# Gate and up projections by seven products of quarters instead of eight, in a two-layer decoder trunk

## The chip, the core and the metric

The kernel runs on one core of a Trainium2 chip. The metric is the device time of one execution in microseconds; lower is better. The core has five engines that run their own queues of instructions in order and wait for one another through semaphores: TensorE (PE in the profile; its weight loads are PEld), VectorE (DVE), ScalarE (ACT), GpSimd (POOL) and SyncE (SP), which here only issues DMA transfers. Matmul results land in PSUM, in 8 banks of 128 x 512 fp32; everything else lives in SBUF, in tiles of 128 partitions.

## The reference

One sequence of 512 tokens of width 1024 goes through two layers. Layer 0 mixes tokens with a short gated convolution and sliding-window attention, layer 1 with gated linear attention and latent attention. Each mixer is followed by a layer norm of `ALPHA * x + y`, by a SwiGLU feed-forward part of width 2816, and by another layer norm. The change concerns the feed-forward part:

```python
def swiglu(x, w_gate, w_up, w_down):
    return (jax.nn.silu(x @ w_gate) * (x @ w_up)) @ w_down
```

with x of 512 x 1024, `w_gate` and `w_up` of 1024 x 2816 and `w_down` of 2816 x 1024, all fp32.

## The kernel before

**Products in three passes.** TensorE multiplies in the type float32r, which holds fewer bits than fp32. So each fp32 operand is split in a high and a low part: `split` rounds it on ScalarE (`hi`), and takes `src - hi` on VectorE (`lo`), or on GpSimd for the first three weights after a `down`. A product is then hi·hi + hi·lo + lo·hi, three matmuls.

**Weights** lie in one DRAM tensor as pieces of 128 x 1024 fp32 (512 KB) in the order of their use. `weight()` loads the next piece into a `raw` tile (pool of 5; issued on SP) and splits it into a `w` tile (pool of 5, each with both parts). A load waits for its `raw` tile to be free, that is for the split of an earlier weight.

**Input of the feed-forward part.** `layer_norm` makes one block of 128 tokens at a time, and its `flip` transposes the block on TensorE (8 transposes into two PSUM tiles). ScalarE casts them to `xh` and VectorE makes `xl`: both hold x transposed, 128 x 8 x 512 (features k of the input in eights, tokens along the row). The norm's reciprocal root, `rs`, is a pow on GpSimd.

**Gate and up** (`ffn`). 22 feature tiles of 128 features; each needs a gate and an up product, and each of these 8 (k) x 3 matmuls of 512 columns (`gemm_a`), whose lhsT is 128 x 128 of the weight and whose rhs is `xh` or `xl`. Tiles 0 and 1 run in two halves of 256 tokens, so that the first halves can start while the last two blocks of the norm are still being made: with the first halves are woven the flips of the third and fourth block. `finish` makes the hidden tile `h` = silu(gate) · up with a tanh on ScalarE and two operations on VectorE.

**Down.** For each of the 22 hidden tiles, split on the way into two `hx` tiles, 4 x 2 x 3 matmuls of 512 columns; then the norm.

**Order.** Only TensorE's queue follows the order of the program's text. For the other engines a scheduler decides, by the dependencies and its own costs, before the program is built.

**Names.** `wk` are 14 slots, which hold hidden tiles; `m8` is one tile of 8 x 512 that holds the mixer's output and then eight hidden tiles; `tmp` and `p` are temporaries of four buffers each; `ps` are PSUM banks. Lines that matter below: L176 matmuls of `gemm_a`; L281 matmuls of `down`; L94 and L100 the two parts of `split`, L98 its GpSimd form; L231 to L255 the norm, with L249 the pow and L255 its last step; L263 to L268 the flip.

Of the kernel before, what the change touches and what calls it, by code (L numbers as in the profile page):

```python
# [10 lines left out]
F32 = mybir.dt.float32  # L11
F32R = mybir.dt.float32r
# [20 lines left out]
WARM = 8  # L33
RAW, WP, WK, HX = 5, 5, 14, 11
LEVELS = (64, 32, 16, 8, 4, 2, 1)
# [8 lines left out]
def trunk(ctx, tc, a, out):  # L44
# [31 lines left out]

    def small(shape, tag):
        return sm.tile(shape, F32, tag=tag, name=nm(tag))

# [44 lines left out]
    def begin(banks):  # L124
# [98 lines left out]

    def layer_norm(b, acc, gb, last):

# [33 lines left out]
        def flip():  # L259
            for h in range(2):  # L260
                tp = ps()
                for k in range(4):
                    nc.tensor.transpose(tp[:, k * P:(k + 1) * P],  # L263
                                        xn[:, b, h * 512 + k * P:h * 512 + (k + 1) * P], ident)
                tv = tp.rearrange("p (k t) -> p k t", k=4)
                dst = (slice(None), slice(4 * h, 4 * h + 4), slice(b * P, (b + 1) * P))
                nc.scalar.copy(out=xh[dst], in_=tv)
                tt(out=xl[dst], in0=tv, in1=xh[dst].bitcast(F32), op=ALU.subtract)  # L268
        return flip

    def down(hs, groups, gb, last=False, after=None):

# [18 lines left out]
        for gi, size in enumerate(groups):  # L291
            parts = [prep(k) for k in range(k0, k0 + size)]
            k0 += size
            for b in range(NB):
                if gi == 0:
                    acc[b] = [ps(), ps()]
                todo = [(part, h) for part in parts for h in range(2)]
                if k0 == nk:
                    todo.sort(key=lambda x: x[1])
                for n, ((k, hh, hl, w), h) in enumerate(todo):  # L300
                    if n == 6 * len(todo) // 10 and k0 == nk and b >= 2 and not last:
                        flips.pop(0)()
                    one(k, b, h, hh, hl, w)
                if gi == 0 and after:
                    after.pop(0)()
                if k0 == nk:
                    flips.append(layer_norm(b, acc[b], gb, last))
        state["pool"] = POOL
        return flips

    def ffn(layer, last, flips):
        gb = load_ln("ffn", layer)
        m8 = big.tile([P, 8, S], F32, tag="m8", name=nm("m8"))
        hs = []

        def finish(f, pg, pu):
            h = m8[:, f, :] if f < 8 else slot()
            t = temp()
# [7 lines left out]
        for f in range(2):  # L326
            for part in range(2):
# [4 lines left out]
                gemm_a(bank, w, cols=slice(0, 256), ks=range(4, KD))  # L332
                first.append((w, bank))
        for f in range(2):
            for w, bank in first[2 * f:2 * f + 2]:
                gemm_a(bank, w, cols=slice(256, 512))
            finish(f, first[2 * f][1], first[2 * f + 1][1])
        with tc.issue_after(norm.ins):
            w = weight()
        for f in range(2, KF):  # L340
            pg, pu = ps(), ps()
            gemm_a(pg, w or weight())
            w = None
            gemm_a(pu, weight())
            finish(f, pg, pu)
        return down(hs, [1] * (KF - 5) + [5], gb, last)


    def mixer0():
# [120 lines left out]
        weave(att[1:], fill[4:])  # L470
        return down([mix[:, i, :] for i in (4, 5, 6, 7, 0, 1, 2, 3)], [4, 4], gb)

# [8 lines left out]
    def mixer1(flips):  # L481
# [7 lines left out]
        def latent(b, bank):  # L489
# [352 lines left out]
        for c in range(3):  # L842
# [11 lines left out]
        return down([mix[:, i, :] for i in (4, 5, 6, 7, 0, 1, 2, 3)], [4, 4], gb,  # L854
                    after=[lambda: output_flip(2), lambda: output_flip(3)])

# [26 lines left out]
def _chunks(w_in0, w_out0, w_in1, w_out1, wg, wu, wd, uq, ukv):  # L883
# [120 lines left out]
```

## Time and profile before

| | |
|---|---|
| median of 3 runs | 1114.32 us (1113.13 to 1114.58) |
| profiled execution | 1115.11 us, its span 1113.3 us |
| TensorE | busy 1098.2 us (99%), 5488 matmuls |
| VectorE | 549.7 us (49%) |
| ScalarE | 374.3 us (34%) |
| GpSimd | 79.3 us (7%) |
| DMA | 109.18 MB, mean 98 GB/s |

"Busy" counts the time in which an engine has an instruction running. Matmuls overlap in the array, so that the mean length of one is longer than the pitch at which they follow one another; how fast they run is read from their starts. A chain of work, followed back from the last instruction, tells which engine's time made the end.

### The profile page before, as it was taken

To read this page: it belongs to the slowest core of one execution; us is meant where nothing else is said; L and a number is where in the kernel's file an instruction comes from. 1 tells how busy PE (TensorE), PEld (TensorE's weight loads), DVE (VectorE), ACT (ScalarE), POOL (GpSimd) and SP (SyncE) were. 2 spreads that over 40 slices of the span, in tenths; PEclk is the share of its full clock that TensorE was granted. 3 is DMA by queue.
4 is the path that set the end of the run, shared out by engine and by line. 5 is a ranking of instruction groups with operands and counts; after the bars stand their busy time and mean duration, and the time that the engine had idled before them with its cause. 6 is when DMAs were issued, how large, how long until landed. Compare 5 with 4: busy or idle time off the path is not lost.

```text
span 1113.3 us, 13695 instructions
## 1 busy us (share of the span) xinstructions
PE 1098.2 (99%) x5488; PEld 918.8 (83%) x5488; DVE 549.7 (49%) x910; ACT 374.3 (34%) x656; POOL 79.3 (7%) x108
## 2 busy tenths in 40 slices
PE   9999999999999999999999999999999999999997
PEld 7888889888888888888987788889888888888885
DVE  5666458433333333334857885485433333333337
ACT  4543343322222222323466444343322222223321
POOL 0000013000000000000513411130000000000001
PEclk9999999999999999999999999999999999999999
DMA  9512223422222322221341030314222223232202
GB/s 353 180 64 77 76 76 114 133 95 94 95 98 94 108 99 95 95 95 57 95 152 58 1 115 9 122 59 170 96 95 95 95 95 102 95 106 96 95 1 76
DMA packets 31487, 109.18 MB, mean 98 GB/s; under 512 B 3504, under 2 KB 3648, under 8 KB 31424
## 3 DMA queue, kind: packets, MB, share of 16 engines
q1 hardware_dynamic: 31424, 108.31, 28.8%
q8 instruction: 43, 0.70, 0.3%
q14 instruction: 20, 0.16, 0.1%
HBM read 106.20 MB, written 2.10 MB: 97 GB/s over the span
## 4 chain that ended last, share of the span: by engine, by line
PE 91%; DVE 6%; ACT 1%; issue 1%; DMA 0%; POOL 0%; DVEq 0%; SPq 0%; ACTq 0%; POOLq 0%
PE ps L176 52%; PE ps L281 26%; PE ps L210 6%; DVE xn L255 1%; PE ps L733 1%; DVE p L252 1%; DVE p L231 1%; PE ps L657 1%; DVE xl L268 1%; PE ps L431 1%; PE ps L378 1%; PE ps L418 1%; DVE w L100 1%; DVE st L234 1%; PE ps L785 0%
## 5 line engine op out<-in xcount | busy, mean ns | idle before, releaser
L176 PE MATMUL ps<-xh,w 128*128 128x512 f32 (+1 forms) x1888 | 556.9, 377 | 0.8 <-ACT xh L94 0.8
L176 PEld LDWEIGHTS ps<-xh,w 128*128 128x128 f32 x1888 | 347.5, 189 | 66.2 <-ACT xh L94 1.5
L176 PE MATMUL ps<-xl,w 128*128 128x512 f32 (+1 forms) x944 | 354.9, 376 | 0.5 <-DVE xl L268 0.5
L281 PE MATMUL ps<-w,hx 128*128 128x512 f32 x1440 | 329.4, 390 | 0.0
L281 PEld LDWEIGHTS ps<-w,hx 128*128 128x128 f32 x1440 | 269.7, 188 | 55.6
L94 ACT CAST w<-raw 128x1024 fp32r<-128x1024 f32 (+2 forms) x184 | 189.8, 1039 | 343.5 <-PE ps L281 160.4
L100 DVE TENSOR_TENSOR w<-raw,w 128x1024 fp32r<-128x1024 f32 (+1 forms) x175 | 212.6, 1218 | 73.2 <-ACT w L94 68.7
L176 PEld LDWEIGHTS ps<-xl,w 128*128 128x128 f32 x944 | 178.3, 189 | 32.8 <-DVE xl L268 0.9
L320 DVE SCALAR_TENSOR_TENSOR tmp<-tmp,ps 128x512 f32<-128x512 f32 x44 | 30.3, 688 | 152.2 <-ACT tmp L319 152.2
L319 ACT ACTIVATE tmp<-ps 128x512 f32<-128x512 f32 x44 | 26.3, 598 | 180.4 <-PE ps L176 180.4
L249 POOL TENSOR_TENSOR rs<-ve,neghalf 128x1 f32<-128x1 f32 x16 | 11.5, 719 | 741.8 <-DVE ve L247 711.3
L100 DVE TENSOR_TENSOR hx<-wk,hx 128x512 fp32r<-128x512 f32 x28 | 19.4, 692 | 82.8 <-PE ps L281 82.8
L210 PE MATMUL ps<-w,xh 128*128 128x512 f32 (+1 forms) x192 | 58.1, 383 | 0.0
L321 DVE SCALAR_TENSOR_TENSOR wk<-tmp,ps 128x512 f32<-128x512 f32 x28 | 19.3, 688 | 74.1 <-PE ps L176 74.1
L100 DVE TENSOR_TENSOR hx<-m,hx 128x512 fp32r<-128x512 f32 x32 | 21.7, 686 | 45.8 <-PE ps L281 37.5
L210 PEld LDWEIGHTS ps<-w,xh 128*128 128x128 f32 x192 | 35.5, 188 | 5.3
L98 POOL TENSOR_TENSOR w<-raw,w 128x512 fp32r<-128x512 f32 (+1 forms) x18 | 28.1, 1594 | 154.9 <-ACT w L94 153.1
L210 PE MATMUL ps<-w,xl 128*128 128x512 f32 (+1 forms) x96 | 36.3, 378 | 0.0
L231 DVE SCALAR_TENSOR_TENSOR p<-xn,ps 128x512 f32<-128x512 f32 x32 | 21.8, 680 | 15.6 <-PE ps L281 15.6
L252 DVE SCALAR_TENSOR_TENSOR p<-p,neg,lng 128x512 f32<-128x512 f32 x32 | 25.8, 826 | 5.9 <-ACT ps L245 5.9
L255 DVE SCALAR_TENSOR_TENSOR xn<-p,rs,lnb 128x512 f32<-128x512 f32 x32 | 26.7, 876 | 2.0 <-POOL rs L249 1.4
L321 DVE SCALAR_TENSOR_TENSOR m<-tmp,ps 128x512 f32<-128x512 f32 x16 | 11.0, 688 | 32.1 <-PE ps L176 31.8
(178 smaller groups left out, 650.4 us busy)
## 6 DMA issues: line engine op xcount, KB each, us to landing
raw<-in_w_dram SPq DMA_DIRECT2D x182, 512.0 KB, 3.6
hx<-in_xT_dram SPq DMA_DIRECT2D x8, 256.0 KB, 5.5
xn<-in_xn_dram SPq DMA_DIRECT2D x4, 512.0 KB, 8.4
out_dram<-xn SPq DMA_DIRECT2D x8, 256.0 KB, 2.0
raw<-in_w_dram SPq DMA_DIRECT2D x4, 256.0 KB, 5.2
lng<-in_ln_mix_g_dram SPq DMA_DIRECT2D x2, 512.0 KB, 6.8
lnb<-in_ln_mix_b_dram SPq DMA_DIRECT2D x2, 512.0 KB, 6.8
lng<-in_ln_ffn_g_dram SPq DMA_DIRECT2D x2, 512.0 KB, 4.4
```

The lines of the kernel that those rows point to most:

```text
L94: nc.scalar.copy(out=hi, in_=src)
L98: nc.gpsimd.tensor_tensor(out=lo[:, c], in0=src[:, c], in1=hi[:, c].bitcast(F32), op=ALU.subtract)
L100: tt(out=lo, in0=src, in1=hi.bitcast(F32), op=ALU.subtract)
L176: mm(dst[:, cols], lhsT=l[:, k, :], rhs=r[:, k, cols], start=(k == 0 and n == 0), stop=(k == KD - 1 and n == 2))
L210: mm(banks[b][:, :n], lhsT=l[:, k, t], rhs=r[:, c], start=(k == 0 and m == 0), stop=(k == KD - 1 and m == 2))
L231: stt(out=r[h], in0=xn[:, b, h * 512:h * 512 + 512], scalar=ALPHA, in1=acc[h], op0=ALU.mult, op1=ALU.add)
L252: stt(out=r[h], in0=r[h], scalar=neg, in1=g[:, hs], op0=ALU.add, op1=ALU.mult)
L255: state["ln"] = stt(out=xn[:, b, hs], in0=r[h], scalar=rs, in1=be[:, hs], op0=ALU.mult, op1=ALU.add)
L281: mm(acc[b][h], lhsT=l[:, bs], rhs=r[:, h * 512:h * 512 + 512], start=(k == 0 and n == 0), stop=(k == nk - 1 and n == 2))
L319: act(out=t, in_=pg, func=AF.Tanh, scale=0.5)
L320: stt(out=t, in0=t, scalar=1.0, in1=pg, op0=ALU.add, op1=ALU.mult)
L321: stt(out=h, in0=t, scalar=0.5, in1=pu, op0=ALU.mult, op1=ALU.mult)
```

## The change

In `ffn` the feature tiles 2 to 21 change; tiles 0 and 1 stay as they were.

**Seven products.** Two feature tiles are taken together (a pair), gate and up at once. The input is cut in quarters: A11, A12 (first 256 tokens, first and second half of the input features) and A21, A22 (last 256 tokens). The weights of a pair are cut likewise: G0, G1 (gate, first and second half of the input features) and U0, U1 (up). Each quarter of a pair is 128 x 1024 fp32, so again a piece of 512 KB. The four results (gate and up, first and last tokens) are by definition eight products of quarters. The new code forms them from seven, in Winograd's variant of Strassen's scheme, with the sign of up turned over, so that all sums of weights are plain additions:

| product | weight | input | PSUM bank |
|---|---|---|---|
| 0 | G0 + U0 | S1 = A22 - A21 | b |
| 1 | G0 + U0 + U1 | S2 = -(S1 + A11) | d |
| 2 | G0 | A11 | a |
| 3 | U0 + U1 | S3 = A11 - A21 | c |
| 4 | G1 | A12 | a, added |
| 5 | U1 | S4 = S1 + A11 - A12 | b, added |
| 6 | G0 + U0 + U1 + G1 | A22 | c, added |

A product is 2 tiles x 4 (k) x 3 passes = 24 matmuls of 256 columns, whose results for both tiles lie side by side in one bank. VectorE and ScalarE combine the banks (`take`).

**Sums of the weights.** `t` is loaded with G0, and a DMA from GpSimd's queue adds U0 to it in SBUF (`accum_op`); `u` is U0 with U1 added in the same way; before product 1 VectorE adds U1 (`y`) to `t`; later a third such DMA adds G1 to `t`. So a pair has five plain loads (`t`, `y`, `u`, `x` = G0, `z` = G1) on SP and three accumulating ones on GpSimd.

**Sums of the input.** `layer_norm` before a feed-forward part gets `keep`: after the flip ScalarE copies the fp32 transposed block once more, to `xT` (in the `m8` slot). `sums` makes S1, S4 and S3 in twelve `hx` tiles, and `last_sum` writes S2 over the halves of `xh` and `xl` that hold A21, after tiles 0 and 1 have read them.

**Order.** Within `sevens` one written order holds for all five engines: step i issues the loads due, makes the weight of product i (`make`), and takes product i - 4 (`AHEAD = 4`).

**Around it.** `hx` has 12 buffers instead of 11. The small gate weight of layer 1's mixer is no longer held from the start: it is loaded there, into a `wk` slot, and stands on SP right ahead of the load of the cosine table. Hidden tiles 0 to 13 are now in `wk`, 14 to 21 in `m8`.

```diff
-RAW, WP, WK, HX = 5, 5, 14, 11
+RAW, WP, WK, HX = 5, 5, 14, 12
+AHEAD = 4
+DIRECT = 2
...
+                if keep:
+                    nc.scalar.copy(out=keep()[dst], in_=tv)
...
+    def piece(i, out, add=False):
+        src = a["w"][i // 2, :, (i % 2) * D:(i % 2) * D + D]
+        if add:
+            nc.gpsimd.dma_start(out=out, in_=src, accum_op=ALU.add)
+        else:
+            nc.sync.dma_start(out=out, in_=src)
+
+    def sums():
...
+        for j in range(2):
+            lo_k, hi_k = slice(2 * j, 2 * j + 2), slice(4 + 2 * j, 6 + 2 * j)
+            a11, a21 = xT[:, lo_k, :256], xT[:, lo_k, 256:]
+            a12, a22 = xT[:, hi_k, :256], xT[:, hi_k, 256:]
+            q, r = three(temp()), three(temp("p"))
+            tt(out=q, in0=a22, in1=a21, op=ALU.subtract)
+            split(q, out["s1"][0][j], out["s1"][1][j])
+            tt(out=q, in0=q, in1=a11, op=ALU.add)
+            tt(out=r, in0=q, in1=a12, op=ALU.subtract)
+            split(r, out["s4"][0][j], out["s4"][1][j])
+            r = three(temp("p"))
+            tt(out=r, in0=a11, in1=a21, op=ALU.subtract)
+            split(r, out["s3"][0][j], out["s3"][1][j])
+            late.append(q)
+
+        def last_sum():
+            for j in range(2):
+                h, l = out["s2"][0][j], out["s2"][1][j]
+                act(out=h, in_=late[j], func=AF.Copy, scale=-1.0)
+                stt(out=l, in0=late[j], scalar=-1.0, in1=h.bitcast(F32), op0=ALU.mult, op1=ALU.subtract)
+        return out, last_sum
...
+        sx, last_sum = sums()
         for f in range(2):
             for w, bank in first[2 * f:2 * f + 2]:
                 gemm_a(bank, w, cols=slice(256, 512))
             finish(f, first[2 * f][1], first[2 * f + 1][1])
-        with tc.issue_after(norm.ins):
-            w = weight()
-        for f in range(2, KF):
-            pg, pu = ps(), ps()
-            gemm_a(pg, w or weight())
-            w = None
-            gemm_a(pu, weight())
-            finish(f, pg, pu)
+        last_sum()
+        sevens(sx, hs, hidden_tile)
...
+            for at, args in ((-4, ("t", 0)), (-3, ("t", 1, True)), (-2, ("y", 2)), (-2, ("u", 1)),
+                             (-1, ("u", 2, True)), (-1, ("x", 0)), (1, ("z", 3)), (2, ("t", 3, True))):
+                loads.setdefault(7 * p + at, []).append((p, *args))
+
+        def make(i):
+            p, pos = divmod(i, 7)
+            src = raw[p, "ttxuzyt"[pos]]
+            if pos == 1:
+                tt(out=src, in0=src, in1=raw[p, "y"], op=ALU.add)
+            hi, lo = pair()
+            split(src, hi, lo)
...
+        def product(bank, w, x, start=True):
+            hi, lo = w
+            for f in range(2):
+                for k in range(4):
+                    for m, (l, r) in enumerate(((hi, x[0]), (hi, x[1]), (lo, x[0]))):
+                        mm(bank[:, f * 256:f * 256 + 256], lhsT=l[:, f, k, :], rhs=r[k // 2][:, k % 2, :],
+                           start=(start and f == 0 and k == 0 and m == 0), stop=(k == 3 and m == 2),
+                           skip_group_check=True)
...
+        with tc.manual_schedule(engines={E.PE, E.Activation, E.DVE, E.Pool, E.SP}):
+            for i in range(n + AHEAD):
+                for args in loads.get(i, ()):
+                    fetch_quarter(*args)
+                if i < n:
+                    make(i)
+                if i >= AHEAD:
+                    take(i - AHEAD)
...
+        wgate = slot()[0:16, :256]
+        nc.sync.dma_start(out=wgate, in_=a["wgate"])
```

In `take` a product's bank is combined with the temporaries `s`, `p5`, `p7` and `up0`: per pair three copies out of PSUM and two tanh on ScalarE, seven operations of 512 columns and four of 256 on VectorE.

**The new order, place 1: VectorE at the fourth block's norm of layer 0.** Rows of before first: `st`, `mv`, `neg`, `ve`, the two rows each of L252 and L255 are the norm; `xl` from two `ps` are the flips, first of the third block, then of the fourth; `w` from `raw` is a weight's split.

```order
L234 BN_STATS st_1586<-p_1585 128x6
L239 BN_AGGR mv_1593<-st_1586 128x2
L240 TENSOR_SCALAR neg_1587<-mv_1593 128x1
L241 TENSOR_SCALAR ve_1588<-mv_1593 128x1
L252 SCALAR_TENSOR_TENSOR p_1584<-p_1584,neg_1587,lng_415 128x512
L252 SCALAR_TENSOR_TENSOR p_1585<-p_1585,neg_1587,lng_415 128x512
L255 SCALAR_TENSOR_TENSOR xn<-p_1584,rs_1597,lnb_416 128x512
L255 SCALAR_TENSOR_TENSOR xn<-p_1585,rs_1597,lnb_416 128x512
L268 TENSOR_TENSOR xl<-ps_1658,xh 128x4x128
L268 TENSOR_TENSOR xl<-ps_1665,xh 128x4x128
L100 TENSOR_TENSOR w_1865<-raw_1863,w_1865 128x1024
L268 TENSOR_TENSOR xl<-ps_1733,xh 128x4x128
```

The same place after; `w_1931` is the weight of product 0, and L431 adds U1 to it for product 1.

```order
L237 BN_STATS st_1595<-p_1594 128x6
L104 TENSOR_TENSOR w_1931<-raw_1919,w_1931 128x1024
L242 BN_AGGR mv_1602<-st_1595 128x2
L271 TENSOR_TENSOR xl<-ps_1666,xh 128x4x128
L243 TENSOR_SCALAR neg_1596<-mv_1602 128x1
L244 TENSOR_SCALAR ve_1597<-mv_1602 128x1
L271 TENSOR_TENSOR xl<-ps_1674,xh 128x4x128
L255 SCALAR_TENSOR_TENSOR p_1593<-p_1593,neg_1596,lng_419 128x512
L255 SCALAR_TENSOR_TENSOR p_1594<-p_1594,neg_1596,lng_419 128x512
L258 SCALAR_TENSOR_TENSOR xn<-p_1593,rs_1606,lnb_420 128x512
L258 SCALAR_TENSOR_TENSOR xn<-p_1594,rs_1606,lnb_420 128x512
L431 TENSOR_TENSOR raw_1919<-raw_1919,raw_1922 128x1024
```

A split and the third block's two `xl` have moved ahead of the norm's last steps, and a sum stands where a split stood ahead of the fourth block's `xl`.

**Place 2: ScalarE where tiles 0 and 1 end and the seven products begin.** Before, tanh (L319) and casts of weights alternate.

```order
L319 ACTIVATE tmp_1807<-ps_1614 128x512
L94 CAST w_1896<-raw_1894 128x1024
L94 CAST w_1931<-raw_1929 128x1024
L94 CAST hx_3157<-m_1607 128x512
L319 ACTIVATE tmp_1859<-ps_1690 128x512
L94 CAST w_1960<-raw_1958 128x1024
L94 CAST w_1995<-raw_1993 128x1024
```

After, from the tanh of tile 1 (L378) on: `w_1946` and `w_1950` are the weights of products 3 and 4, L359 the upper parts of S2, `hx` from `p` casts for S4 and S3, L458 the first copy out of bank b.

```order
L378 ACTIVATE tmp_1911<-ps_1700 128x512
L98 CAST w_1946<-raw_1924 128x1024
L359 ACTIVATE xh<-tmp_1783 128x2x256
L359 ACTIVATE xh<-tmp_1796 128x2x256
L98 CAST w_1950<-raw_1934 128x1024
L98 CAST hx_1776<-p_1797 128x512
L98 CAST hx_1780<-p_1805 128x512
L458 COPY p_1958<-ps_1954 128x512
```

S2 stands behind the weight of product 3 and ahead of the casts for the second halves of S4 and S3. On VectorE the lower part of S4's second half comes ahead of the first lower part of S2, and that of S3 between the two of S2.

**Place 3: GpSimd at the same norm.** Before:

```order
L98 TENSOR_TENSOR w_1610<-raw_1608,w_1610 128x512 x2
L249 TENSOR_TENSOR rs_1439<-ve_1429,neghalf 128x1
L249 TENSOR_TENSOR rs_1483<-ve_1473,neghalf 128x1
L249 TENSOR_TENSOR rs_1540<-ve_1531,neghalf 128x1
L98 TENSOR_TENSOR w_1641<-raw_1639,w_1641 128x512 x2
L98 TENSOR_TENSOR w_1686<-raw_1684,w_1686 128x512 x2
L249 TENSOR_TENSOR rs_1597<-ve_1588,neghalf 128x1
```

After, with the accumulating DMAs (L325):

```order
L102 TENSOR_TENSOR w_1618<-raw_1616,w_1618 128x512 x2
L325 DMA raw_1919<-in_w_dram 128x1024
L252 TENSOR_TENSOR rs_1443<-ve_1433,neghalf 128x1
L252 TENSOR_TENSOR rs_1487<-ve_1477,neghalf 128x1
L252 TENSOR_TENSOR rs_1547<-ve_1538,neghalf 128x1
L102 TENSOR_TENSOR w_1649<-raw_1647,w_1649 128x512 x2
L102 TENSOR_TENSOR w_1696<-raw_1694,w_1696 128x512 x2
L325 DMA raw_1924<-in_w_dram 128x1024
L252 TENSOR_TENSOR rs_1606<-ve_1597,neghalf 128x1
```

The first accumulation (U0 to `t`) is issued ahead of the first norm's pow, the second (U1 to `u`) ahead of the fourth's; each waits there for the plain load that it adds to.

More of the change, by code (lines that the diff above doesn't have):

```diff
@@ L75, in temp, with small @@
         return tmp.tile([P, 512], dt, tag=tag, name=nm(tag))
-    def small(shape, tag):
-        return sm.tile(shape, F32, tag=tag, name=nm(tag))
+    def small(shape, tag, pool=None):
+        return (pool or sm).tile(shape, F32, tag=tag, name=nm(tag))
     def ps():
@@ L222, in load_ln, with layer_norm @@
         return g, b
-    def layer_norm(b, acc, gb, last):
+    def layer_norm(b, acc, gb, last, keep=None):
         g, be = gb
@@ L268, in flip, with down @@
                 tt(out=xl[dst], in0=tv, in1=xh[dst].bitcast(F32), op=ALU.subtract)
+                if keep:
+                    nc.scalar.copy(out=keep()[dst], in_=tv)
         return flip
-    def down(hs, groups, gb, last=False, after=None):
+    def down(hs, groups, gb, last=False, after=None, keep=None):
         nk = len(hs)
@@ L306, in down, with whole @@
                 if k0 == nk:
-                    flips.append(layer_norm(b, acc[b], gb, last))
+                    flips.append(layer_norm(b, acc[b], gb, last, keep))
         state["pool"] = POOL
         return flips
+    def whole():
+        if "xT" not in state:
+            state["xT"] = big.tile([P, KD, S], F32, tag="m8", name=nm("m8"))
+        return state["xT"]
+    def piece(i, out, add=False):
[4 more added lines that the diff above has]
+            nc.sync.dma_start(out=out, in_=src)
@@ new lines, in sums, with three @@
+    def sums():
+        xT = state.pop("xT")
+        out = {n: ([slot2(F32R), slot2(F32R)], [slot2(F32R), slot2(F32R)]) for n in ("s1", "s4", "s3")}
+        out = {n: [[t.rearrange("p (k t) -> p k t", k=2) for t in half] for half in hl] for n, hl in out.items()}
+        out["s2"] = [[t[:, 2 * j:2 * j + 2, 256:] for j in range(2)] for t in (xh, xl)]
+        def three(t):
+            return t.rearrange("p (k t) -> p k t", k=2)
+        late = []
+        for j in range(2):
[18 more added lines that the diff above has]
+        return out, last_sum
@@ L311, in ffn, with hidden_tile @@
     def ffn(layer, last, flips):
         gb = load_ln("ffn", layer)
-        m8 = big.tile([P, 8, S], F32, tag="m8", name=nm("m8"))
         hs = []
+        m8 = {}
+        def hidden_tile(f):
+            if f < WK:
+                return slot()
+            if not m8:
+                m8["t"] = big.tile([P, 8, S], F32, tag="m8", name=nm("m8"))
+            return m8["t"][:, f - WK, :]
         def finish(f, pg, pu):
-            h = m8[:, f, :] if f < 8 else slot()
+            h = hidden_tile(f)
@@ L470, in mixer0 @@
         weave(att[1:], fill[4:])
-        return down([mix[:, i, :] for i in (4, 5, 6, 7, 0, 1, 2, 3)], [4, 4], gb)
+        return down([mix[:, i, :] for i in (4, 5, 6, 7, 0, 1, 2, 3)], [4, 4], gb, keep=whole)
     def rms_scale(ss, n, w):
@@ L854, in mixer1 @@
         return down([mix[:, i, :] for i in (4, 5, 6, 7, 0, 1, 2, 3)], [4, 4], gb,
-                    after=[lambda: output_flip(2), lambda: output_flip(3)])
+                    after=[lambda: output_flip(2), lambda: output_flip(3)], keep=whole)
     neghalf = const.tile([P, 8], F32, name="neghalf")
@@ L904, in ffn @@
     def ffn(layer):
-        for f in range(KF):
+        for f in range(DIRECT):
             feat(wg[layer][:, f * P:(f + 1) * P])
             feat(wu[layer][:, f * P:(f + 1) * P])
+        for f in range(DIRECT, KF, 2):
+            for w, half in ((wg, 0), (wu, 0), (wu, 1), (wg, 1)):
+                quarter = w[layer][half * 512:half * 512 + 512, f * P:(f + 2) * P]
+                pieces.append(quarter.reshape(4, P, 2, P).transpose(1, 2, 0, 3).reshape(P, D))
         rows(wd[layer])
```

77 lines of the change are left out of this document (72 added, 5 removed).

## The prediction

> **What bounds the kernel now.** I read the page first, then the chain that ended last in order of time, then the groups by form, then the timelines of single engines.
>
> ```profile
> span 1113.3 us, 13695 instructions
> ...
> PE 1098.2 (99%) x5488; PEld 918.8 (83%) x5488; DVE 549.7 (49%) x910; ACT 374.3 (34%) x656; POOL 79.3 (7%) x108
> ...
> PEclk9999999999999999999999999999999999999999
> ...
> q1 hardware_dynamic: 31424, 108.31, 28.8%
> ...
> PE 91%; DVE 6%; ACT 1%; issue 1%; DMA 0%; POOL 0%; DVEq 0%; SPq 0%; ACTq 0%; POOLq 0%
> ...
> 188.09 229.28 PE ps L176 x1055
> ...
> 756.47 229.29 PE ps L176 x1055
> ```
>
> TensorE carries 91% of the chain, at full granted clock. The last two rows are the gate and up products of the two layers: one unbroken stretch of matmuls each, 229.3 us, with no wait in it. The other engines have slack there:
>
> ```profile
> core 0: us, PE busy (x) PEld busy (x) DVE busy (x) ACT busy (x) POOL busy (x), PEclk, DMA share, GB/s
> 205.00:405.00 200.00, 200.00 (x884) 165.64 (x884) 72.60 (x77) 50.24 (x60) 0.00 (x0) 1.00 0.29 95
> ```
>
> So this stretch is worth what its matmuls cost, as long as VectorE (36% busy), ScalarE (25%), the idle GpSimd and the DMA engines (29%) keep up with what the change gives them.
>
> **Fewer, narrower matmuls.** A pair of feature tiles takes 2 x 2 x 8 x 3 = 96 matmuls of 512 columns before, and 7 x 2 x 4 x 3 = 168 of 256 columns after. That is 7/8 of the columns only if a half-width matmul takes half the time. The durations in the groups (391 and 284 ns) include a pipeline's latency and can't be used; the pitch from start to start can. Columns: start, length, engine, line, tile, form, count in a row.
>
> ```profile
> 198.99 0.28 PE L176 MATMUL ps<-xl,w 128*128 128x256 f32 x1
> 199.11 0.40 PE L176 MATMUL ps<-xh,w 128*128 128x256 f32 x2
> 199.35 0.28 PE L176 MATMUL ps<-xl,w 128*128 128x256 f32 x1
> ...
> 333.12 0.39 PE L176 MATMUL ps<-xl,w 128*128 128x512 f32 x1
> 333.35 0.62 PE L176 MATMUL ps<-xh,w 128*128 128x512 f32 x2
> 333.80 0.39 PE L176 MATMUL ps<-xl,w 128*128 128x512 f32 x1
> ```
>
> Three matmuls of 256 columns go from 198.99 to 199.35, 120.0 ns each; three of 512 columns from 333.12 to 333.80, 226.7 ns each. The narrow ones load the same full weight for each matmul as the new products will, so 120 ns holds for them. A pair costs 96 x 0.2267 = 21.76 us before and 168 x 0.120 = 20.16 us after: 1.60 us saved, not the 2.72 of a pure eighth, since each matmul carries some 13 ns that don't shrink. Ten pairs in two layers: 20 x 1.60 = **-32.0 us**.
>
> [...]
>
> **What VectorE and ScalarE get for a pair.** Seven splits of a weight instead of four, one added sum of 1024 columns, and eleven operations of at most 512 columns that combine the products (before: four).
>
> ```profile
> 148.90 1.22 DVE L100 TENSOR_TENSOR w<-raw,w 128x1024 fp32r<-128x1024 f32 x1
> 150.04 0.68 DVE L100 TENSOR_TENSOR hx<-m,hx 128x512 fp32r<-128x512 f32 x1
> 150.64 1.22 DVE L100 TENSOR_TENSOR w<-raw,w 128x1024 fp32r<-128x1024 f32 x1
> ...
> 171.69 3.89 ACT L94 CAST w<-raw 128x1024 fp32r<-128x1024 f32 x4
> ...
> 165.56 1.05 ACT L267 CAST xh<-ps 128x512 fp32r<-128x512 f32 x2
> ```
>
> By pitch, VectorE takes 1.14 us for 1024 columns and 0.60 for 512: 8 x 1.14 + 11 x 0.60 = 15.7 us at most. ScalarE: 7 x 0.97 + 5 x 0.53 = 9.4 us. Both stay under the 20.16 us of TensorE. Weights are split four products (4 x 24 x 0.12 = 11.5 us) ahead, so a wait of an in-order engine for one product's end is covered as well. I cost this at nothing; its cover is the 4.5 us that VectorE has left in each pair.
>
> **The transfers.** Five plain loads and three accumulating ones replace four loads. No row of this trace shows an accumulating transfer.
>
> ```profile
> raw<-in_w_dram SPq DMA_DIRECT2D x182, 512.0 KB, 3.6
> ...
> DMA to landing us min/median/max: 3.0/3.6/11.3
> ```
>
> Queue q1 moved 108.31 MB in 28.8% of 1113.3 us, 338 GB/s while busy, so a plain 512 KB takes 1.55 us of the 16 engines. An accumulating one is bounded below by the same 1.55 us, and above by about three times that, 4.65 us, if reading the source, reading the destination and writing it don't overlap. I take twice, 3.1 us, since it reads twice as many bytes as the load that is its nearest row. A pair then needs 5 x 1.55 + 3 x 3.1 = 17.1 us of DMA, 85% of 20.16; at the lower end 12.4, at the upper 21.7. As to latency, the tightest is the third accumulation: it starts after the split of the second product's weight and is needed five products later, 14.4 us, less about 3 us for the splits themselves. Even the longest landing above, 11.3 us, fits in that. GpSimd issues three of these in 20 us and does nothing else there. Cost taken: nothing, covered by those 11 us; both ends go into the range.
>
> **The start of each layer's products.** Here the change adds work to a chain that is not TensorE's.
>
> ```profile
> 180.16 1.13 DVE w L100
> ...
> 183.18 0.52 issue
> ...
> 185.11 1.20 DVE xl L268 x2
> 186.31 1.13 DVE w L100
> 187.44 0.61 DVE xl L268
> ...
> 185.26 1.04 PE L263 MATMUL ps<-pack,xn 128*128 128x128 f32 x8
> ...
> 188.09 0.39 PE L176 MATMUL ps<-xl,w 128*128 128x256 f32 x1 [0.25 <-DVE xl L268]
> ```
>
> Before, VectorE finishes the fourth block's norm at 185.11, and TensorE's transposes begin at 185.26 without a gap. After, the split of the first product's weight (+1.13) and both xl of the third block (+1.20, moved up, not added) stand ahead of that norm, the 0.52 wait for GpSimd's rs falls away, and the sum of the second product's weight (1.13) takes the place of the split at 186.31. The xl on which TensorE waited at 188.09 comes 1.13 us later, with some latency **+1.2 us** a layer. ScalarE's eight added copies of a transposed half (0.53 each) lie beside this, except the last two: they follow the last xl and hold up the fp32 sums of the input.
>
> Then the second halves of tiles 0 and 1 run, 96 x 0.12 = 11.5 us. In this time VectorE makes S1, S3, S4 (fourteen operations of 0.60) and two weight splits; by its order S1 is ready some 2.5 us before they end. S2 is not: it overwrites the xh and xl that these matmuls read, so it starts after them. ScalarE then does two halves of S2 (2 x 0.53), a weight cast (0.97) and a cast for S4 (0.53) before VectorE, which in its order must first finish S4's second half, reaches S2's lower parts: about 0.25 + 1.06 + 0.97 + 0.53 + 0.15 + 2 x 0.60 = 4.2 us until the first, another 1.2 us until the second. The first product covers 24 x 0.12 = 2.9 us, and six matmuls of the second run on the first half alone. The second product ends about **1.75 us** late, per layer. Ends: 0, if that order overlaps better, and 5 us.
>
> GpSimd's queue: the accumulation ahead of the first norm is issued when its load lands, some 3.6 us after the last split of the mixer's weights (150.64 + 1.14), so by 156.
>
> ```profile
> 160.50 0.54 POOL L249 TENSOR_TENSOR rs<-ve,neghalf 128x1 f32<-128x1 f32 x1 [6.24 <-DVE ve L247]
> ...
> 173.19 6.92 POOL L98 TENSOR_TENSOR w<-raw,w 128x512 fp32r<-128x512 f32 x4
> 182.47 1.05 POOL L249 TENSOR_TENSOR rs<-ve,neghalf 128x1 f32<-128x1 f32 x1 [2.36 <-DVE ve L241]
> ```
>
> The norm's pow comes at 160.50; the second accumulation stands between the splits that end at 180.1 and a pow that will now come near 184. Both have over 3 us for an issue whose nearest rows are 0.33 us (a load on SP) and 1.7 us (half a split on GpSimd): nothing.
>
> **The gate weight of layer 1's mixer** is now loaded where the cosine table is, at 574.47, and that table takes 3.9 us to land.
>
> ```profile
> 574.47 0.42 SPq L584 DMA_DIRECT2D wk<-in_qcos_dram  x1
> ...
> wk<-in_qcos_dram SPq DMA_DIRECT2D x1, 256.0 KB, 3.9
> ...
> 577.32 0.29 PEld L551 LDWEIGHTS ps<-tmp,wgate 16*128 16x128 f32 x2 [0.35 <-issue]
> ...
> 578.86 1.27 ACT L552 ACTIVATE p<-ps,pack 128x512 f32<-128x512 f32 x2
> ```
>
> It lands near 578.4 against a need at 577.32; the reader of the result starts only at 578.86. Between 0 and 1.1 us; I take **+0.7**.
>
> **Sum.** 1113.3 - 32.0 + 2 x 1.2 + 2 x 1.75 + 0.7 = 1087.9 us of span. The profiled execution took 1115.11 us, 1.8 over its span, and 0.8 over the median of 1114.32, so 1087.9 + 1.8 - 0.8 = **1089 us**. Alone, this case reaches from 1082 (no stall at the starts) to 1096 (these stalls doubled). A measurement of this kernel tells 0.2% (2.2 us) from no change.
>
> **Rivals.** *The DMA engines become the bound* (slower). For: from 12.4 to 21.7 us of 20.16 a pair, with the price of an accumulation unknown. It decides where one takes over 4.1 us of the engines, (20.16 - 7.75)/3; the gain is gone at 4.5, and at 4.65 or more a pair takes at least 21.7 us: 20 x 1.55 = +31, 1120 us and up. [...] Chance 0.15.
>
> *Accumulations land late, without full engines.* VectorE stops at a split, and behind it in its queue stand the sums that free PSUM banks. Beyond 11 us each further microsecond costs up to 20 us a run: 1097 to 1116. For: GpSimd and VectorE hinder one another in this trace:
>
> ```profile
> 175.49 3.48 DVE L255 SCALAR_TENSOR_TENSOR xn<-p,rs,lnb 128x512 f32<-128x512 f32 x2
> ...
> 183.70 1.41 DVE L255 SCALAR_TENSOR_TENSOR xn<-p,rs,lnb 128x512 f32<-128x512 f32 x2
> ```
>
> The same operation takes 3.48 us beside GpSimd's splits and 1.41 without. Against: three issues in 20 us. Chance 0.17, of which 0.03 ends within 0.2%.
>
> *VectorE becomes the bound*: by the same rows, if its 15.7 us grew by half, 23.6 us a pair, +68 us, 1157. It decides at a growth of 28%. 0.02.
>
> *Weight loads become the bound.* If they didn't overlap, the 165.64 us of PEld for 884 loads, 187 ns each, would set the pitch: 168 x 0.187 = 31.4 us a pair, +193 us, 1282. The rows at 199 us, at 120 ns with a full load each, speak against it: 0.01. [...]
>
> *More is saved*: at best a narrow matmul takes half the pitch of a wide one, 113.3 ns, as where matmuls of one form run on for long the 13 ns might hide; 168 x 20 x 0.0067 = 22 us less, down to 1067. Against: the 95 narrow ones in a row here keep 120. 0.05.
>
> **Chances.** The forecast 0.60, the rivals as above. Faster 0.60 + 0.14 + 0.05 = 0.79, same 0.03, slower 0.15 + 0.02 + 0.01 = 0.18. The range from 1079 to 1113 takes in the forecast, the late accumulations that still end faster, and the upper part of the last case.
>
> **What would show it.** The unbroken stretch of matmuls should be 168 x 0.12 us a pair, about 202 us in ten pairs, with a gap of 1 to 3 us after its first product and none after; VectorE near 75% there, DMA near 85%; the fourth block's transposes 1 to 2 us late. I'm wrong if VectorE's splits wait for a DMA in steady state, if the pitch isn't 120 ns, or if the DMA share stands at 100%.

## The result: slower by 1.5%, the products right, a ring of transfers missed

The changed kernel takes 1131.44 us (median of 4 runs, 1127.23 to 1134.19) against 1114.45 before in the same session: ratio 1.0152, 95% interval 1.0119 to 1.0185. I had forecast 1089 us, faster. Its profiled execution took 1130.84 us, span 1129.1, at a granted clock of 0.985 (before: 0.997).

The page of the changed kernel: busy time by engine, the two queues, the chain that ended last by engine and by line, and the issues of the weights' transfers with their median time to landing.

```profile
span 1129.1 us, 17311 instructions
...
PE 1083.4 (96%) x6928; PEld 972.5 (86%) x6928; DVE 715.9 (63%) x1162; ACT 478.9 (42%) x808; POOL 128.9 (11%) x168
...
q1 hardware_dynamic: 34304, 118.80, 31.0%
q0 software_dynamic: 8640, 31.46, 16.7%
...
PE 51%; DMA 20%; DVE 16%; issue 7%; ACT 5%; POOL 0%; ACTq 0%; DVEq 0%; POOLq 0%; SPq 0%
...
raw<-in_w_dram SPq DMA_DIRECT2D x202, 512.0 KB, 5.0
raw<-in_w_dram POOLq DMA_DIRECT2D x60, 512.0 KB, 6.0
```

TensorE's share of the chain fell from 91% to 51%; transfers, VectorE and ScalarE took its place. The stretch of the seven products can be cut at VectorE's sums (L431, one a pair). Four of the eight windows of layer 0, pair by pair, and the sum of all eight; columns: length, busy time of each engine, granted clock, DMA share.

```profile
240.10:264.98 24.88, 20.65 (x169) 20.25 (x169) 15.08 (x20) 9.40 (x12) 2.59 (x3) 1.00 0.76 187
264.98:286.55 21.57, 21.57 (x169) 21.57 (x169) 15.07 (x20) 9.39 (x12) 2.59 (x3) 0.92 0.65 171
286.55:308.63 22.08, 20.74 (x171) 20.34 (x170) 15.08 (x21) 9.50 (x12) 2.59 (x3) 1.00 0.79 194
308.63:330.09 21.46, 20.66 (x170) 20.25 (x170) 15.08 (x21) 9.40 (x12) 2.59 (x3) 1.00 0.78 195
...
sum 183.15, PE 169.76 PEld 167.32 DVE 120.59 ACT 75.57 POOL 20.71; mean PE 21.22 PEld 20.92 DVE 15.07 ACT 9.45 POOL 2.59
```

Eight pairs take 183.15 us, 22.9 each, where 20.16 were forecast and 21.76 were needed before. No engine and no queue is full: VectorE works 15.07 us of 22.9, the DMA share is 0.65 to 0.83. So something goes round. The chain of that stretch, in order of time, shows what:

```profile
244.91 1.15 DVE w L104
246.08 6.22 DMA raw<-in_w_dram
...
252.94 9.14 DMA raw<-in_w_dram
262.12 0.04 issue
262.16 1.05 ACT w L98
...
264.98 1.23 DVE raw L431
...
269.79 1.14 DVE w L104
```

At 244.91 VectorE splits `x`, the third product's weight, which frees a raw buffer. The five buffers then hold `t`, `u`, `y`, `z` and this one, so only now can the next pair's `t` be loaded (6.22), only then accumulated (9.14), and only then can VectorE and ScalarE make the weights of products 0, 1 and 2, the last of which, at 269.79, frees the next buffer. This loop is called the ring below. One round took 24.9 us: 16.1 from the start of the load to the first cast behind the accumulation, and 8.8 for what VectorE and ScalarE then do (two casts, three splits, a sum and three combining operations). In the best rounds, such as the one from 314.6 to 336.0, it took 21.4: 5.0 for the load, 0.6 until the accumulation is issued, 7.0 for the accumulation, and again 8.8. (In some rounds the chain puts the start of the accumulation down to VectorE's L493 just before; in the four rounds from 246 to 328 us the load landed about 0.6 us ahead of it.) A lead of four products is no help against a ring; it only delays the first wait.

TensorE feels it through ScalarE's queue. The timeline of ScalarE, and that of TensorE just after:

```profile
305.81 1.04 ACT L98 CAST w<-raw 128x1024 fp32r<-128x1024 f32 x1 [5.71 <-DMA raw<-in_w_dram]
306.76 0.58 ACT L468 COPY p<-ps 128x512 f32<-128x512 f32 x1
```

```profile
263.74 0.39 PE L444 MATMUL ps<-xh,w 128*128 128x256 f32 x1 [4.04 <-ACT p L468]
...
264.80 0.60 PE L444 MATMUL ps<-xh,w 128*128 128x256 f32 x2
...
268.18 3.06 PE L444 MATMUL ps<-hx,w 128*128 128x256 f32 x24
...
307.39 0.39 PE L444 MATMUL ps<-xh,w 128*128 128x256 f32 x1 [1.23 <-ACT p L468]
...
352.64 0.38 PE L444 MATMUL ps<-xh,w 128*128 128x256 f32 x1 [2.95 <-ACT p L468]
...
398.02 0.58 PE L444 MATMUL ps<-xh,w 128*128 128x256 f32 x1 [2.07 <-ACT p L468]
```

The cast of the next pair's `t` waits 5.71 us for its transfer, and behind it stands the copy of bank c (L468), without which the last product, which adds to c, can't start.

### The profile page after: what moved, and what is told of

It reads as the page before. It is cut to its first block, busy times and chain, and to the rows that moved or that the text cites. A ratio compares the mean times of both kernels' runs of the same rounds, so it can differ in the third digit from the quotient of the medians.

```text
span 1129.1 us, 17311 instructions
## 1 busy us (share of the span) xinstructions
PE 1083.4 (96%) x6928; PEld 972.5 (86%) x6928; DVE 715.9 (63%) x1162; ACT 478.9 (42%) x808; POOL 128.9 (11%) x168
## 3 DMA queue, kind: packets, MB, share of 16 engines
q0 software_dynamic: 8640, 31.46, 16.7%
## 4 chain that ended last, share of the span: by engine, by line
PE 51%; DMA 20%; DVE 16%; issue 7%; ACT 5%; POOL 0%; ACTq 0%; DVEq 0%; POOLq 0%; SPq 0%
PE ps L286 26%; DMA raw<-in_w_dram 19%; PE ps L179 10%; PE ps L213 5%; DVE w L104 4%; ACT w L98 4%; PE ps L444 3%; DVE raw L431 2%; DVE xn L258 1%; DVE tmp L474 1%; DVE p L475 1%; DVE p L255 1%; PE ps L745 1%; DVE p L234 1%; DVE xl L271 1%
## 5 line engine op out<-in xcount | busy, mean ns | idle before, releaser
L104 DVE TENSOR_TENSOR w<-raw,w 128x1024 fp32r<-128x1024 f32 (+1 forms) x235 | 282.3, 1217 | 164.1 <-ACT w L98 159.3
L98 ACT CAST w<-raw 128x1024 fp32r<-128x1024 f32 (+2 forms) x244 | 249.3, 1039 | 207.7 <-DMA raw<-in_w_dram 122.8
L444 PE MATMUL ps<-xh,w 128*128 128x256 f32 x1280 | 251.1, 291 | 26.8 <-ACT p L468 24.2
L444 PEld LDWEIGHTS ps<-xh,w 128*128 128x128 f32 x1280 | 210.7, 198 | 31.7 <-ACT p L468 27.1
L444 PE MATMUL ps<-xl,w 128*128 128x256 f32 x640 | 185.5, 290 | 0.5 <-DVE xl L360 0.5
L444 PE MATMUL ps<-hx,w 128*128 128x256 f32 x1440 | 182.5, 283 | 0.0
L444 PEld LDWEIGHTS ps<-hx,w 128*128 128x128 f32 x1440 | 177.3, 192 | 0.0
L179 PE MATMUL ps<-xh,w 128*128 128x512 f32 (+1 forms) x608 | 161.2, 349 | 1.1 <-ACT xh L98 1.1
L444 PEld LDWEIGHTS ps<-xl,w 128*128 128x128 f32 x640 | 126.9, 198 | 1.3 <-DVE xl L360 1.3
L179 PEld LDWEIGHTS ps<-xh,w 128*128 128x128 f32 x608 | 106.3, 189 | 17.1 <-ACT xh L98 1.9
L179 PE MATMUL ps<-xl,w 128*128 128x512 f32 (+1 forms) x304 | 104.9, 345 | 0.2 <-DVE xl L104 0.2
L325 POOL DMA_DIRECT2D raw<-in_w_dram x60 | 52.1, 868 | 402.9 <-DVE w L104 150.9
L252 POOL TENSOR_TENSOR rs<-ve,neghalf 128x1 f32<-128x1 f32 x16 | 10.7, 669 | 301.5 <-DVE ve L250 271.6
```

The lines of the kernel that those rows point to most:

```text
L98: nc.scalar.copy(out=hi, in_=src)
L104: tt(out=lo, in0=src, in1=hi.bitcast(F32), op=ALU.subtract)
L179: mm(dst[:, cols], lhsT=l[:, k, :], rhs=r[:, k, cols], start=(k == 0 and n == 0), stop=(k == KD - 1 and n == 2))
L325: nc.gpsimd.dma_start(out=out, in_=src, accum_op=ALU.add)
L444: mm(bank[:, f * 256:f * 256 + 256], lhsT=l[:, f, k, :], rhs=r[k // 2][:, k % 2, :], start=(start and f == 0 and k == 0 and m == 0), stop= ...
```

## The experiments

Three theories. *Ring*: the loop above sets the pace. *Traffic*: the DMA engines are full in effect. *Order*: ScalarE's copies stand behind casts that wait, so writing them ahead cures it. All times are medians; every ratio is to the kernel before, in the same session. The last column is the steady distance between VectorE's sums in layer 0.

| kernel | us | ratio, 95% interval | a pair, us |
|---|---|---|---|
| changed kernel | 1131.44 | 1.0152 [1.0119, 1.0185] | 22.9 |
| z last | 1088.04 | 0.9768 [0.9753, 0.9782] | 20.16 |
| no first accumulation | 1086.71 | 0.9758 [0.9743, 0.9772] | 20.16 |
| no third accumulation | 1086.84 | 0.9759 [0.9745, 0.9774] | 20.16 |
| copies ahead of splits | 1159.88 | 1.0433 [1.0400, 1.0466] | 24.8 |
| x one place earlier | 1097.01 | 0.9847 [0.9833, 0.9862] | 20.7 |
| no third, t one place later | 1174.51 | 1.0541 [1.0525, 1.0557] | 25.2 |
| plain transfers for accumulations | 1087.94 | 0.9765 [0.9749, 0.9782] | 20.16 |
| z last, copies ahead | 1088.31 | 0.9766 [0.9752, 0.9781] | 20.16 |
| sums on VectorE | 1153.86 | 1.0359 [1.0345, 1.0373] | 24.0 |
| sums on VectorE, a step earlier | 1088.00 | 0.9772 [0.9756, 0.9788] | 20.16 |
| z last, gate weight early | 1086.54 | 0.9754 [0.9740, 0.9767] | - |
| z last, again | 1087.31 | 0.9761 [0.9748, 0.9774] | - |

**z last.** The products of `y` and `t` move up and that of `z` (with its tanh) goes last, so `z` needs its buffer later and the next `t` takes the free fifth buffer at once.

```diff
-((-4, ("t", 0)), (-3, ("t", 1, True)), (-2, ("y", 2)), (-2, ("u", 1)),
- (-1, ("u", 2, True)), (-1, ("x", 0)), (1, ("z", 3)), (2, ("t", 3, True)))
+((-7, ("t", 0)), (-5, ("t", 1, True)), (-3, ("u", 1)), (-2, ("y", 2)),
+ (-1, ("u", 2, True)), (-1, ("x", 0)), (3, ("z", 3)), (2, ("t", 3, True)))
...
-            src = raw[p, "ttxuzyt"[pos]]
+            src = raw[p, "ttxuytz"[pos]]
```

> Same transfers, same sums, same five buffers as the changed kernel; only the order within a pair of tiles differs: the product of the fourth quarter alone (z) comes last instead of fifth, so the free fifth buffer takes the next pair's t some five products earlier. Theory 1 (a ring: split of x frees a buffer, load of the next t, its accumulation, its splits, and again; 21.4 to 25 us a pair against TensorE's 20.16): the ring is cut, a pair falls to about 20.2 to 20.6 us, 1088 to 1100 us, VectorE no longer waits for transfers in the middle of the stretch. Theory 2 (the DMA engines are full in effect, three accumulations at 3.1 us each): the traffic is the same, so no gain, 1125 to 1136 us. Theory 3 (ScalarE's copies out of PSUM stand behind casts that wait): half of the loss stays, 1105 to 1120 us.

Measured 1088.04 us. Windows of this kernel, one pair each, and four of its groups of matmuls (L444 the seven products, L266 the flips, L716 the gate; at the end the idle time before them and what ended it):

```profile
213.56:233.72 20.16, 20.16 (x171) 20.16 (x170) 15.34 (x21) 9.91 (x13) 2.62 (x3) 1.00 0.88 209
...
274.04:294.19 20.15, 20.15 (x171) 20.15 (x170) 15.33 (x20) 9.89 (x13) 2.62 (x3) 1.00 0.91 212
...
sum 161.28, PE 161.28 PEld 161.28 DVE 122.63 ACT 79.22 POOL 20.80; mean PE 20.16 PEld 20.16 DVE 15.33 ACT 9.90 POOL 2.60
```

```profile
L444 PE MATMUL ps<-xh,w 128*128 128x256 f32 x1280 | 237.1, 283 | 0.0
...
L444 PE MATMUL ps<-xl,w 128*128 128x256 f32 x640 | 181.5, 284 | 0.5 <-DVE xl L360 0.5
...
L266 PE MATMUL ps<-pack,xn 128*128 128x128 f32 x96 | 13.3, 275 | 3.3 <-DVE xn L258 2.3 <-issue 1.1
...
L716 PE MATMUL ps<-tmp,wk 16*128 16x512 f32 x4 | 1.9, 606 | 1.1 <-DMA wk<-in_wgate_dram 1.1
```

A pair takes 20.16 us to the hundredth, with all three accumulations and a DMA share that has risen to 0.81 to 0.91. Traffic falls as the cause, and so does the order of copies, which was not touched.

**No first, and no third accumulation.** Each drops one entry of the table of loads.

```diff
-(-3, ("t", 1, True)),        (no first)
-(2, ("t", 3, True))          (no third)
```

> The first accumulation of each pair (second quarter onto t) is left out, so the sums of weights are not the right ones; everything else as in the changed kernel. Theory 1: this accumulation of 7 to 9 us stands in the ring; without it the ring is about 5.6 + 8.9 = 14.5 us, under 20.16, and the time falls to 1088 to 1100 us. Theory 2: a third of the accumulating traffic (3.1 of 17.1 us of the DMA engines a pair) goes, 1108 to 1122 us, and the same as in no_third. Theory 3: the casts that wait are fewer, 1100 to 1115 us.

> The third accumulation of each pair (fourth quarter onto t) is left out instead, the one that the prediction called the tightest; its sums are not the right ones. Theory 1: it isn't in the ring, 1118 to 1132 us (a little less than the changed kernel only because the other transfers have less company). Theory 2: same as no_first, 1108 to 1122 us. A third accumulation that is the tightest, as predicted: 1088 to 1100 us.

1086.71 and 1086.84 us: both cure it, though the third is not a link of the ring. My expectation for it (1118 to 1132) was a miss, and alone the two equal times would have spoken for traffic. In the trace without the third, the next `t` loads in 4.5 us and its accumulation lands in 5.7 (the issues at 319.91 and 324.95), where the four rounds of the changed kernel from 246 to 328 us have 4.9 to 6.2 and 7.0 to 9.1.

```profile
raw<-in_w_dram SPq DMA_DIRECT2D x1, 512.0 KB, 4.5
...
raw<-in_w_dram POOLq DMA_DIRECT2D x1, 512.0 KB, 5.7
```

The ring is then 4.5 + 0.6 + 5.7 + 8.8 = 19.6 us, just under 20.16. So it was near its edge, and company on the DMA engines moved it over. The next two runs were made to decide between this and traffic.

**x one place earlier, all accumulations kept.** The second and third product change places, so the buffer of `x` is free one split and one sum earlier.

```diff
-(-4, ("t", 0)), ... (2, ("t", 3, True))
-src = raw[p, "ttxuzyt"[pos]];  if pos == 1: (t + y)
+(-5, ("t", 0)), ... (3, ("t", 3, True))
+src = raw[p, "txtuzyt"[pos]];  if pos == 2: (t + y)
```

> Against the changed kernel only the second and the third product of each pair change places: the weight x is split one place earlier, so its buffer is free one split and one sum earlier for the next pair's t; all transfers and accumulations stay. The ring theory, with what the first four runs taught (the ring is near TensorE's 20.16 us: 5.0 load + 7.0 accumulation + 9 of splits = 21.4 with the third accumulation beside it, some 19 without): the ring loses about 3.5 us of VectorE and ScalarE, comes to some 18 us, and the whole loss goes: 1086 to 1095 us. The theory that the third accumulation itself is late: it now starts one product later and is needed at the same place, so no gain or a loss, 1125 to 1145 us.

1097.01 us: most of the loss goes, but 9 us stay, 2 more than I allowed. GpSimd's timeline:

```profile
311.36 1.75 POOL L325 DMA_DIRECT2D raw<-in_w_dram  x2 [7.25 <-DVE w L104]
322.82 0.86 POOL L325 DMA_DIRECT2D raw<-in_w_dram  x1 [9.71 <-DMA raw<-in_w_dram]
331.44 1.75 POOL L325 DMA_DIRECT2D raw<-in_w_dram  x2 [7.76 <-DVE w L104]
```

The next `t` has landed by 310.3, but its accumulation stands behind the pair's third in GpSimd's queue, which waits for a split until 311.1; both then run together, and land after 5.6 (the third) and 8.9 us. The ring stays at some 20.6 us.

**No third accumulation, t one place later.** The opposite test: without the third, but `y` takes the buffer that `x` frees and `t` waits for that of `u`.

```diff
-(-4, ("t", 0)), (-3, ("t", 1, True)), (-2, ("y", 2)), ... (2, ("t", 3, True))
+(-4, ("y", 2)), (-3, ("t", 0)), (-2, ("t", 1, True)), ...
```

> The third accumulation is left out (its sums aren't the right ones), and the next pair's t is loaded one place later: y takes the buffer that x frees, t the one that u frees. The ring theory: some 19 us plus one split, 21.5 us a pair, so the loss comes back without the third accumulation: 1105 to 1130 us. The theory that the third accumulation, or the traffic, is the cause: 1085 to 1090 us as without the shift.

1174.51 us, the slowest of all, with less traffic than the changed kernel. Windows of this kernel, and its issues in the stretch from 216 to 416 us:

```profile
297.01:322.31 25.30, 20.67 (x167) 20.26 (x167) 15.07 (x20) 9.39 (x12) 1.72 (x2) 0.98 0.54 146
322.31:348.09 25.78, 21.89 (x169) 21.69 (x168) 15.07 (x20) 9.39 (x12) 1.72 (x2) 0.90 0.54 144
```

```profile
raw<-in_w_dram SPq DMA_DIRECT2D x40, 512.0 KB, 4.6
raw<-in_w_dram POOLq DMA_DIRECT2D x16, 512.0 KB, 9.0
```

A DMA share of 0.54 and a loss of 5%: it is the ring, not traffic. I had it at 21.5 us and the time at 1130 at most; it is 25.2, above all because the accumulation lands after 9.0 us instead of 5.7. VectorE's timeline in it suggests why:

```profile
329.57 1.22 DVE L104 TENSOR_TENSOR w<-raw,w 128x1024 fp32r<-128x1024 f32 x1
...
333.49 3.49 DVE L104 TENSOR_TENSOR w<-raw,w 128x1024 fp32r<-128x1024 f32 x3
```

The splits of products 4, 5 and 6 run back to back and free their buffers within 3.5 us, and the loads into these start at 334.73, 335.87 and 337.00, beside the accumulation on which the ring hangs, which is issued at 335.99. The changed kernel has the same row (319.81, x3, 3.49). In the kernel without the third accumulation, where TensorE doesn't wait in this stretch, the same three splits start 1.5 and 2.4 us apart (304.95, 306.44, 308.88). So a wait seems to bunch the transfers that make the next wait longer; no run tests this by itself.

**Plain transfers for accumulations.**

```diff
-            nc.gpsimd.dma_start(out=out, in_=src, accum_op=ALU.add)
+            nc.gpsimd.dma_start(out=out, in_=src)
```

> All three accumulations become plain transfers of the same bytes on the same queue, so the sums of weights are left out. The ring theory: a plain transfer lands in some 4.5 us in place of 7, the ring falls to about 18.5 us, 1085 to 1092 us; the landings tell the price of accumulating.

1087.94 us. The landings of the 25 transfers on GpSimd's queue between 216 and 416 us, first with plain ones, then accumulating in the kernel with z last, where TensorE doesn't wait either:

```profile
raw<-in_w_dram POOLq DMA_DIRECT2D x25, 512.0 KB, 4.8
...
raw<-in_w_dram POOLq DMA_DIRECT2D x25, 512.0 KB, 8.7
```

In the changed kernel the accumulating ones have a median of 5.8 us there.

**The order of copies**, in the changed kernel and in the one with z last.

```diff
-                if i < n:
-                    make(i)
                 if i >= AHEAD:
                     take(i - AHEAD)
+                if i < n:
+                    make(i)
```

> In each step the products and the copies out of PSUM are written ahead of the split of a weight, so that ScalarE and VectorE empty a bank before they turn to a weight that may wait for a transfer; nothing is removed. Theory 1: the ring of transfers and splits stays as long, 1122 to 1140 us. Theory 2: the same, 1125 to 1136 us. Theory 3 (in-order copies behind waiting casts are what TensorE waits for): 1092 to 1108 us.

> Both earlier edits together: the fourth quarter's product last, and the copies out of PSUM written ahead of the split in each step. Ring theory: the ring is cut and the order ahead of it matters little, 1086 to 1095 us. If the order of copies and splits costs time by itself (take_first lost 29 us against the changed kernel): 1100 to 1120 us.

1159.88 and 1088.31 us. With the ring, writing the copies ahead costs 28 us more, and worse than I expected of either theory; without it, nothing. So the order was how TensorE felt the ring, not the cause. That the extra 28 us are waits for TensorE's products, now in the ring, is argued, not shown.

**Sums on VectorE.** No accumulations: four loads and four sums a pair, in two orders.

```diff
+            if pos in (0, 1, 3, 6):
+                a_, b_ = {0: "xu", 1: "ty", 3: "uy", 6: "tz"}[pos]
+                tt(out=src, in0=raw[p, a_], in1=raw[p, b_], op=ALU.add)
...                          (a step earlier: in make(i), for product i + 1, ahead of split i;
                              products "txtuyzt", sums at 0, 2, 3, 6)
```

> No accumulating transfers: each quarter is loaded once, and the four sums of a pair are VectorE's (t = x + u, t + y, u + y, t + z); the fourth quarter's product comes after the third quarter's, and five buffers stay. VectorE gets 3 x 1.14 us more a pair, 15.3 + 3.4 = 18.7 us of TensorE's 20.16; the ring has one load of some 4 us and no accumulation. Theory of the ring: 1086 to 1093 us. The prediction's rival that VectorE becomes the bound: it decides where VectorE's order leaves it less than 20.16 us of work that can run on, 1095 to 1120 us.

> As dve_sums (no accumulating transfers, four sums a pair on VectorE), but each sum is written one step earlier, ahead of the split of the weight before it, and the products x and t + y change places so that this can be done. In dve_sums VectorE was busy 18.6 us a pair but stood 4 x 1.17 us in each between a sum and the split of it, while ScalarE cast the sum: 24.0 us. Theory of the round trip: these waits go, 18.6 + 0.7 = 19.3 us stay under 20.16, 1085 to 1093 us. Theory that VectorE's own work is the bound (operations that lengthen one another): 1125 to 1155 us.

1153.86 and 1088.00 us. The first lies beyond both of my ranges for it. VectorE's timeline in the first:

```profile
312.04 1.22 DVE L433 TENSOR_TENSOR raw<-raw,raw 128x1024 f32<-128x1024 f32 x1
...
314.43 1.23 DVE L104 TENSOR_TENSOR w<-raw,w 128x1024 fp32r<-128x1024 f32 x1 [1.17 <-ACT w L98]
...
316.17 1.22 DVE L433 TENSOR_TENSOR raw<-raw,raw 128x1024 f32<-128x1024 f32 x1
...
318.56 1.22 DVE L104 TENSOR_TENSOR w<-raw,w 128x1024 fp32r<-128x1024 f32 x1 [1.17 <-ACT w L98]
```

Each sum is followed by a stand of 1.17 us, while ScalarE casts it, before VectorE can split it: 18.6 busy + 4 x 1.17 + 0.7 = 24.0 us, at 77% busy. A step earlier the sums cover these stands, and VectorE runs at 91% (the row below, a window of ten pairs) without holding TensorE up.

```profile
213.00:415.00 202.00, 202.00 (x1637) 199.90 (x1636) 183.89 (x223) 100.57 (x126) 0.00 (x0) 1.00 0.36 116
```

**The gate weight loaded at the start of layer 1's mixer**, with z last.

> The kernel with the fourth quarter's product last, and the gate weight of layer 1's mixer loaded at that mixer's start instead of where its product stands. TensorE waited 1.1 us for it there (the prediction took 0.7). If that is on the path, 1.1 us less than late_z_again, 1086 to 1088 us; if ScalarE's tables after it set the pace, no difference.

> The kernel with the fourth quarter's product last, again, beside late_z_wg: 1088 us, 1.1 us more than late_z_wg if the gate weight's wait is on the path, else the same.

1086.54 against 1087.31 us. The wait of 1.0 us at L716 is gone from the trace and the medians differ by 0.8, but the intervals of the ratios overlap: likely on the path, not settled by times. It has the lowest median of all runs, 28 us under the kernel before.

## Why the prediction failed, by its own steps

**The step that failed** is the sentence on latency: "As to latency, the tightest is the third accumulation ... Cost taken: nothing". I measured each transfer's slack from its start to its use, took the start as given, and compared it with a landing. But a plain load starts when a buffer comes free, and the first accumulation is fed by such a load, so the tightest path was a loop through five buffers: split, load, accumulation, three splits. Its length could have been added up from rows of before and my own 3.1 us of engine time in place of 1.55: 3.6 for the load, 3.6 + 1.55 for the accumulation, and some 9 for two casts, three splits, a sum and three combining operations (2 x 0.97 + 4 x 1.14 + 3 x 0.60 = 8.3, and what lies between), 18 us alone, and more in company. Against 20.16 that leaves 2 us, not 11. The runs showed 21.4 to 24.9 us a round in its place. The prediction's own sign of being wrong, VectorE's splits waiting for a DMA in steady state, is what the trace has: at 305.81 the cast waits 5.71 us for the transfer, and VectorE's split waits for the cast.

**The chance that it would go that way** was in a rival, accumulations that land late without full engines (0.17), but with a price of up to "20 us a run" for each microsecond beyond 11, and thus an upper end of 1116. The price was nearly right: eight pairs take 183.15 us in layer 0 and 182.12 in layer 1 (794.87 to 976.99), so that 16 of the 20 pairs go round at 22.8 to 22.9 us, and 16 x 2.7 = 43 us, against 42.0 between the spans of the changed kernel and z last. The point from which it counts was wrong. Slower matmuls are a small part of this: the granted clock was 0.92, 0.99, 0.93 and 0.97 in four of the eight windows of layer 0 and 1.00 in the others, which makes some 4 of the 21.9 us that these pairs lost. Nor is it shown that they lengthened anything: in 264.98 to 286.55, at 0.92, TensorE never waited, and the window took 21.57 us, about as long as the one from 308.63 at full clock (21.46).

**The DMA engines as the bound** did not come. My 3.1 us for an accumulation was right: 16.7% of 1129.1 us over 60 transfers is 3.14. So was the share, 85%: z last shows 0.81 to 0.91, at full speed.

**Fewer, narrower matmuls**: 120 ns held, and 20.16 us a pair. *VectorE and ScalarE*: 15.33 and 9.90 us a pair against 15.7 and 9.4. Weight loads hid, as the rows had said (in z last they were busy through the same 161.28 us of eight pairs as the matmuls), and no more than forecast was saved. The rival in which they don't hide was added up wrongly: 20 x (31.4 - 20.16) is 225 us on top of 1089, 1314 us, not 1282; its chance was 0.01, and nothing else rests on it.

**The later norm**: TensorE's waits at the flips (L266) rise from 1.1 to 3.3 us, +1.1 a layer; forecast 1.2. **S2**: 0.5 us for both layers instead of 3.5. The latency was right, 4.3 us from the first upper cast to the first lower part (198.20 to 202.54 in the changed kernel), but the cast began before the products of tiles 0 and 1 ended, at 199.33, when the first matmuls of the last one had read their part. **The gate weight**: 1.1 us, the upper end; forecast 0.7.

With these sizes the sum is 1113.3 - 32.0 + 2.2 + 0.5 + 1.1 = 1085.1 us of span, and z last has 1087.1, or 1085.4 when it was run again. The forecast of 1089 us was that of a kernel whose loads come in another order; that z last comes within 1 us of it is in part luck, since the term for S2 was 3.0 us too high.

## What to carry to other kernels

Where a buffer's release starts a load, and the load's data must be worked on before the next release, add up the whole round and compare it with the period of the bound engine; neither busy shares nor a lead of some steps shows it. Take landings from rows with company: the same accumulation landed after 5.7 us in one kernel here and after 9.0 in another. When such a ring is found, try another order in which buffers are needed before giving up the transfers. A sixth buffer, the other obvious remedy, was not run.

## What the runs showed of the hardware

*TensorE's clock halved behind some gaps, for about 3.4 us, and the gap's length alone didn't decide it.* In the changed kernel, after the gap of 4.04 us above, matmuls run at 120 ns for 1 us, then at 213 ns from 264.80 to 268.18, with a granted clock of 0.50 in that window; after 2.95 us the same follows, from 353.57 to 356.98 (0.50), and after 2.07 at once (0.51 from 398.02 to 401.40). After 1.23 us it doesn't (1.00 from 307.39 to 310.80), but neither does it after 2.09 us in the kernel with x one place earlier (776.64 to 778.73), nor after 3.30 us in the one without the third, t one place later (292.47 to 295.77). In z last the clock stays at 1.00 in the stretch of the seven products (216 to 416 us), which has no gap; after the wait of about 1 us for the gate weight it was halved in one profile of this kernel (567.30 to 570.70) and not in the other. The rows: the changed kernel; the stretch after 3.30 us; the two profiles of z last (the last three columns are granted clock, DMA share, GB/s).

```profile
264.80:268.18 3.38, 3.38 (x18) 3.38 (x17) 2.21 (x3) 1.89 (x3) 0.00 (x0) 0.50 0.09 17
...
295.77:299.20 3.43, 3.43 (x28) 3.43 (x29) 2.46 (x3) 0.88 (x1) 0.00 (x0) 1.00 0.27 57
...
566.00:572.00 6.00, 6.00 (x19) 4.66 (x19) 3.69 (x7) 4.48 (x7) 0.00 (x0) 0.72 0.29 89
...
566.00:572.00 6.00, 6.00 (x25) 4.25 (x24) 3.77 (x6) 5.24 (x8) 0.00 (x0) 1.00 0.30 89
```

What decides it was not worked out. Such a gap was paid twice, by the wait and by the slower clock behind it: the 4.04 us were followed by 3.38 us at 0.50, and 2.07 us were enough once.

*An accumulating transfer of 512 KB* costs 3.14 us of the 16 DMA engines in the changed kernel, twice the 1.55 us of a plain one, and lands there after 5.5 to 9.6 us (median 6.0), in z last after 5.3 to 10.6 (median 8.1); issuing it takes GpSimd 0.86 us.
